# Bias loads placed behind weight loads, and a scan buffer returned later, in a two-layer hybrid backbone

## The chip, the cores and the metric

The kernel runs on one core of one Trainium2 chip. The metric is the device time of one execution in microseconds. Each of the runs shown is one execution; their median counts.

## The reference

Two layers work on 256 latent tokens and 256 context tokens of width 1024, all in float32. In each layer one projection of the modulated RMS norm feeds three mixers side by side: a bidirectional diagonal state-space scan (S5), a bidirectional chunked retention with four heads, and a neighbourhood attention with eight heads of 64. Each mixer has a projection of its own and a gate; the gated sum goes through an output projection and a residual, then a SwiGLU FFN follows. Of this the change touches two places. The attention adds a bias per head to the scores inside the window, before one softmax over window and context:

```python
s_win = jnp.einsum('bqhd,brqchd->bhqrc', q_r, k_win).astype(f32) + jnp.transpose(bias, (0, 2, 1, 3))[None]
s_ctx = jnp.einsum('bqhd,bkhd->bhqk', q_r, k_c).astype(f32)
s = jnp.concatenate([s_win.reshape(bsz, H, GRID_W, n_win), s_ctx], axis=-1)
p = jax.nn.softmax(s, axis=-1).astype(v.dtype)
```

The scan of S5 runs over the tokens in both directions and leaves complex states, real and imaginary part, which the readout multiplies.

## The kernel before

Weights come from DRAM as chunks of 128 x 1024 floats, in the order in which the program asks for them. `wraw` loads a chunk into one of four raw buffers in turn, from SyncE's (SP's) queue. `w` then splits it into two fp32r halves, `hi` by a cast on ScalarE (L387) and `lo` by a subtraction on VectorE (L388), in three buffers each. Every product of a projection is three matmuls (`mm3`, L393 to L395). The chunks of the adaLN weights (`ada`) are used as they are, by L526.

A layer is written as generators that `weave` mixes by counts: after each step of a main sequence it takes a set number of steps of side sequences. That fixes the order of the program. The order on each engine and in each queue is then laid out by a planner, which plays the program through with estimated times; `tc.issue_after(ins)` makes it put the instructions of a block behind `ins` on the engine of `ins`. All waits follow from the addresses that are written and read.

Addresses come from `Arena`, which is worked in the order of the program. A normal request takes the first free block behind a cursor that goes round; a request with `top=True` takes the highest block that fits. A buffer that is freed can be given out at once, and its new owner then waits for the old one's readers and writers.

In layer 0 the order is this. Projections of the attention for heads 0 to 3 run with the input of S5 beside them; those for heads 4 to 7 with the scan (`s5_scan`, GpSimd) and `attn(l, 0)`, the attention of heads 0 to 3. Then come the gates of branch 0 with `attn(l, 1)`, heads 4 to 7, and the gates of branch 2 with `s5_out`, the readout. Then `branch_mm(l, 2)` loads the stored gates into `tgm` buffers (L1692); `m_ret` makes the projections of the retention, with the rotary table `rope` (L1456), `s5_glu` and `ret_decay` beside it; and `branch_mm(l, 0)`, `gates(l, 1)` and `retention` follow. Layer 1 has another order of the same parts.

`attn` handles two pairs of heads, m = 0 and 1. For each head it loads the bias (L1397, 128 x 384 floats) into one of the four buffers made in `m_na`, which both halves of the heads share, and turns its sign on ScalarE (L1398). `softmax2` adds it on VectorE (L1334, L1335), takes exponentials on ScalarE (L1340, L1341) and scales (L1346). The result is transposed on PE (L1387), copied (L1411) and multiplied with the values (L1415).

`s5_scan` ends by exchanging halves of the states `X` through the buffer `swap`: two DMAs into it and two copies out of it on GpSimd (L1121, L1122). Layer 0 frees `swap`, `ug` and `X` together in `layer`, ahead of `branch_mm(l, 2)`. `s5_tables(1)` builds layer 1's S5 tables beside layer 0's `m_out`; `b2` is one of them.

Of the kernel before, what the change touches and what calls it, by code (L numbers as in the profile page):

```python
# [199 lines left out]
def mk(ap, off, dims):  # L200
    return bass.AP(ap.tensor, ap.offset + off, [list(ap.ap[0])] + [list(d) for d in dims])
# [29 lines left out]
def chain(*gens):  # L231
    for g in gens:
        yield from g


class Net:
# [451 lines left out]
    def s5_tables(self, l):  # L688

        nc, F = self.nc, self.F  # L690
        if l not in self.tabs:
            self.tabs[l] = F.alloc(1280, "p2", top=True), F.alloc(1040, "BB", top=True)
        P2, bb = (b.ap for b in self.tabs[l])
        for r in range(2):
            for ri in range(2):
                src = mk(self.PW[r * 64:r * 64 + 64], l * 32, [[64, 20], [2, 16], [1, 2]])
                dst = mk(P2[ri * 64:ri * 64 + 64], r * 2, [[64, 20], [4, 16], [1, 2]])
                nc.scalar.copy(dst, src)
        w1, w2 = self.swapped("s5b", l * 1024, 1024, F)
        b2, tm = F.alloc(1024, "b2"), F.alloc(1024, "bbt")  # L700
        f = [P2[:, (ri * 10 + 9) * 64:(ri * 10 + 10) * 64].unsqueeze(2).to_broadcast([P, 64, 16])
             for ri in range(2)]

        def v3(ap):
            return ap.rearrange("p (g h) -> p g h", h=16)

        nc.vector.memset(bb[:, 1024:1040], 0.0)
        for dst, a, b, op in ((bb[:, 0:1024], w1, w2, ALU.add), (b2.ap, w2, w1, ALU.subtract)):
            nc.vector.tensor_tensor(out=v3(dst), in0=v3(a.ap), in1=f[0], op=ALU.mult)
            nc.vector.tensor_tensor(out=v3(tm.ap), in0=v3(b.ap), in1=f[1], op=ALU.mult)  # L710

            x, y = (tm.ap, dst) if b is w2 else (dst, tm.ap)
            nc.vector.scalar_tensor_tensor(out=dst, in0=x, scalar=self.sgn[:, 0:1], in1=y, op0=ALU.mult, op1=op)
        for b in (w1, w2, tm):
            b.free()
        return b2
# [196 lines left out]
    def layer(self, l):  # L913
        nc, F = self.nc, self.F
        last = l == NL - 1
        n = self.nt = 256 if last else 512
        self.n0 = 512 - n
        na = [None, None]
        self.yna = self.yslot[0]
        if l == 0:  # L920
            self.ug = F.alloc(2048, "ug", top=True)
            mu = self.m_u(l)
            for qt in range(1, 4):
                next(mu)
                self.ada2(0, qt)
                next(mu)
                self.modulate(0, 0, [0, 1], self.rb0, 0, range(qt * 2, qt * 2 + 2))
            self.pfree(self.rb0)
            wdma = self.wdma
            for _ in mu:  # L930
                pass
            with self.tc.issue_after(wdma.ins), self.tc.issue_after(self.wdma.ins):
                nc.sync.dma_start(self.xsp, self.xb.ap)
            self.xb.free()
            b2 = self.s5_tables(0)
            ada = self.ada(0, (2, 3, 4, 5))
            self.adas = ada
            self.X = F.alloc(4 * 66 * 16, "X", top=True)
            kw = self.s5_kwins(0, True)
            e_in = chain(*(g for blk in range(4) for g in (self.s5_e(0, b2, blk), self.s5_in(0, blk))))  # L940
            weave(self.m_na(l, 0, na), (e_in, 3))
            self.log_gamma(self.s5in[:, 192:208])
            weave(self.m_na(l, 1, na), (self.s5_scan(l), 18), (self.attn(l, 0, na), 4), (self.take(ada, 5), 1),
                  (self.take(kw, 4), 1))
            weave(self.gates(l, 0, None), (self.attn(l, 1, na), 1.6), (self.take(ada, 5), 0.5), (kw, 0.5))
            weave(self.gates(l, 2, None), (self.s5_out(l, self.yslot[1]), 2), (self.take(ada, 5), 0.5))
            self.swap.free()
            self.ug.free()
            self.X.free()
            self.m = F.alloc(8 * n, "m", top=True)  # L950
            for _ in self.branch_mm(l, 2, None, self.yna, first=True):
                pass
            weave(self.m_ret(l), (self.s5_glu(l, self.yslot[1], self.yslot[0]), 0.8), (self.ret_decay(l), 0.75))
            self.yret = self.yslot[1]
            tg = F.alloc(8 * n, "tg", top=True)
            weave(chain(self.branch_mm(l, 0, None, self.yslot[0]), self.gates(l, 1, tg)), (self.retention(l), 2))
            self.x_alloc()
            nc.sync.dma_start(self.xb.ap, self.xsp)
            for _ in self.branch_mm(l, 1, tg, self.yret, final=True):
                pass  # L960
        else:
            self.norm(l, 0, [2, 3])
            nc.sync.dma_start(self.xsp, self.xb.ap)
            self.xb.free()
            for _ in self.e_left:
                pass
            for b in self.tabs[l]:
                b.free()
            self.ug = F.alloc(2048, "ug", top=True)
            self.X = F.alloc(4 * 66 * 16, "X", top=True)  # L970
            kpre = self.pair([("ws", l, O_NK + m * 128) for m in range(2)])
            for _ in self.m_u(l):
                pass
            weave(self.m_na(l, 0, na, kpre), (chain(*(self.s5_in(l, blk) for blk in range(4)), self.s5_scan(l)), 20))
            ada = self.adas
            weave(self.m_na(l, 1, na), (self.attn(l, 0, na), 2.5))
            self.yret = self.yslot[1]
            weave(self.m_ret(l), (self.attn(l, 1, na), 1.2), (self.ret_decay(l), 0.75))
            self.m = F.alloc(8 * n, "m", top=True)
            weave(self.branch(l, 2, self.yna, 0), (self.retention(l), 2.5))  # L980
            self.swap.free()
            tg = F.alloc(8 * n, "tg", top=True)
            ys5 = self.yslot[0][:, 1024:]
            weave(chain(self.branch(l, 1, self.yret, 1), self.gates(l, 0, tg)),
                  (chain(self.s5_out(l, self.yslot[0]), self.s5_glu(l, self.yslot[0], ys5)), 1))
            self.ug.free()
            self.X.free()
            self.x_alloc()
            nc.sync.dma_start(self.xb.ap, self.xsp)
            for _ in self.branch_mm(l, 0, tg, ys5, final=True):  # L990
                pass
        tg.free()
        self.m.free()
        ada = self.adas
        if last:
            ada = self.ada(1, (5,))
            for _ in self.m_out(l):
                pass
            F.cursor = 8192
            self.norm(l, 1, [2, 3])  # L1000
            self.fill(ada, 2, 1)
            weave(self.ffn(l), (ada, 0.5))
        else:
            e = []

            def ahead():
                self.tabs[1] = F.alloc(1280, "p2", top=True), F.alloc(1040, "BB", top=True)
                for blk in range(4):
                    self.et[blk] = F.alloc(2048, "et", top=True)
                b2 = self.s5_tables(1)  # L1010
                yield
                e.extend(self.s5_e(1, b2, blk) for blk in range(4))
                next(e[0])
                yield

            weave(self.m_out(l, lambda: self.norm(l, 1, [0, 1])), (ahead(), 0.5))
            self.norm(l, 1, [2, 3])

            def rest():
                yield from chain(e[0], e[1], e[2], self.s5_kwins(1))  # L1020
                next(e[3])

            self.adas = self.ada_sum(1, range(5))
            weave(self.ffn(l, lambda: self.norm(l + 1, 0, [0, 1])), (rest(), 0.5), (chain(ada, self.adas), 0.9))
            self.e_left = e[3]
        self.dump(f"xffn{l}", self.xT)
# [338 lines left out]
    def attn(self, l, half, na):  # L1365


        nc, F = self.nc, self.F
# [22 lines left out]
        for m in range(2):  # L1391
            out = self.misc()
            kh, kl, qh, ql = qk[m]
            bias = []
            for h in range(2):
                bias.append(self.biases[m * 2 + h])
                nc.sync.dma_start(bias[h].ap, self.I["nabias"][l, half * 4 + m * 2 + h])  # L1397
                nc.scalar.mul(bias[h].ap, bias[h].ap, -1.0)  # L1398
            val = lambda h, k: nv[:, k, (m * 2 + h) * 64:(m * 2 + h + 1) * 64]
            for qt in range(2):  # L1400
# [443 lines left out]
```

## Time and profile before

| | us |
|---|---|
| median of three runs | 1546.05 |
| fastest and slowest of them | 1538.01 and 1549.89 |
| the profiled execution | 1546.39 |
| its span, first to last instruction | 1544.6 |
| busy in the span: PE, VectorE, ScalarE, GpSimd | 1492.7, 984.1, 626.9, 259.5 |

The mean granted clock of PE over the span is 0.986 of full speed. DMA queues moved 255.35 MB, on average 165 GB/s. The profile names a line of the kernel (L387) for each group of instructions; PE is the matmul side of TensorE, PEld its loading of weights, DVE is VectorE, ACT ScalarE, POOL GpSimd. `fa` is the arena in which all float32 buffers lie, `ra` that of the split halves, `psall` PSUM. Times in rows are microseconds from the start of the span unless they are marked as ns.

### The profile page before, as it was taken

To read this page: it belongs to the slowest core of one execution; us is meant where nothing else is said; L and a number is where in the kernel's file an instruction comes from. 1 tells how busy PE (TensorE), PEld (TensorE's weight loads), DVE (VectorE), ACT (ScalarE), POOL (GpSimd) and SP (SyncE) were. 2 spreads that over 40 slices of the span, in tenths; PEclk is the share of its full clock that TensorE was granted. 3 is DMA by queue.
4 is the path that set the end of the run, shared out by engine and by line. 5 is a ranking of instruction groups with operands and counts; after the bars stand their busy time and mean duration, and the time that the engine had idled before them with its cause. 6 is when DMAs were issued, how large, how long until landed. Compare 5 with 4: busy or idle time off the path is not lost. (4 is left out here: it accounts for less than half of the span.)

```text
span 1544.6 us, 25494 instructions
## 1 busy us (share of the span) xinstructions
PE 1492.7 (97%) x10066; PEld 1269.3 (82%) x10066; DVE 984.1 (64%) x1729; ACT 626.9 (41%) x1121; POOL 259.5 (17%) x612
## 2 busy tenths in 40 slices
PE   7998898999999999999999999999999999999997
PEld 5886676788888888787887788898689899899997
DVE  6884754445356686598599974732565676665666
ACT  4554443334312334332322322454654355444443
POOL 6206996000000000000000000007991000000000
PEclk9999899999999999999999999999999999999999
DMA  9514456873332533455466642432325667555552
GB/s 369 190 55 141 159 208 176 278 258 113 123 102 69 164 96 111 167 186 178 153 205 214 230 160 65 157 123 75 101 83 161 230 225 271 179 192 184 171 190 98
DMA packets 80760, 255.35 MB, mean 165 GB/s; under 512 B 9216, under 2 KB 23040, under 8 KB 77824
## 3 DMA queue, kind: packets, MB, share of 16 engines
q1 hardware_dynamic: 78016, 247.36, 48.4%
q10 hardware_dynamic: 2304, 4.20, 0.8%
q0 software_dynamic: 320, 2.16, 0.6%
q8 instruction: 79, 1.29, 0.3%
q14 instruction: 41, 0.34, 0.1%
HBM read 230.68 MB, written 20.84 MB: 163 GB/s over the span
## 5 line engine op out<-in xcount | busy, mean ns | idle before, releaser
L393 PE MATMUL psall<-ra 128*128 128x256 f32 (+1 forms) x2122 | 711.3, 340 | 6.1 <-ACT ra L387 2.4
L394 PE MATMUL psall<-ra 128*128 128x256 f32 (+1 forms) x2122 | 709.0, 336 | 0.0
L395 PE MATMUL psall<-ra 128*128 128x256 f32 (+1 forms) x2122 | 707.4, 336 | 1.0 <-DVE ra L388 1.0
L388 DVE TENSOR_TENSOR ra<-fa,ra 128x1024 fp32r<-128x1024 f32 (+1 forms) x284 | 344.8, 1216 | 293.1 <-ACT ra L387 285.9
L387 ACT CAST ra<-fa 128x1024 fp32r<-128x1024 f32 (+1 forms) x284 | 293.7, 1038 | 557.9 <-PE psall L394 336.0
L393 PEld LDWEIGHTS psall<-ra 128*128 128x128 f32 x2122 | 401.7, 191 | 63.2 <-issue 10.7
L395 PEld LDWEIGHTS psall<-ra 128*128 128x128 f32 x2122 | 404.0, 191 | 44.9 <-issue 2.7
L394 PEld LDWEIGHTS psall<-ra 128*128 128x128 f32 x2122 | 405.2, 191 | 39.0 <-issue 1.3
L1109 POOL TENSOR_TENSOR fa<-fa 128x64 f32<-128x64 f32 x252 | 106.1, 442 | 137.4 <-ACT fa L1083 127.7
L1064 POOL MEMSET fa<- 128x32 f32 x2 | 0.2, 123 | 730.2 <-DVE ra L846 730.2
L570 DVE SCALAR_TENSOR_TENSOR fa<-fa 128x1024 f32<-128x1024 f32 x70 | 87.6, 1281 | 9.3 <-DMA fa<-in_wst_dram 7.6
L887 PE MATMUL psall<-ra 128*128 128x512 f32 x192 | 77.8, 414 | 0.2 <-ACT fa L1051 0.2
L888 PE MATMUL psall<-ra 128*128 128x512 f32 x192 | 76.2, 397 | 0.0
L1711 DVE SCALAR_TENSOR_TENSOR fa<-psall,fa 128x256 f32<-128x256 f32 x96 | 43.2, 480 | 51.3 <-PE psall L395 51.1
L889 PE MATMUL psall<-ra 128*128 128x512 f32 x192 | 75.3, 399 | 0.3 <-DVE ra L846 0.3
L1112 POOL TENSOR_TENSOR fa<-fa 128x64 f32<-128x64 f32 x126 | 58.2, 462 | 0.0
L1113 POOL TENSOR_TENSOR fa<-fa 128x64 f32<-128x64 f32 x126 | 53.8, 427 | 9.9
L887 PEld LDWEIGHTS psall<-ra 128*128 128x128 f32 x192 | 43.7, 229 | 8.0 <-issue 2.0
L889 PEld LDWEIGHTS psall<-ra 128*128 128x128 f32 x192 | 43.4, 229 | 6.5 <-DVE ra L846 0.8
L756 DVE TENSOR_TENSOR fa<-fa 128x1024 f32<-128x1024 f32 (+1 forms) x32 | 41.1, 1316 | 11.2 <-PE psall L1165 8.8
L888 PEld LDWEIGHTS psall<-ra 128*128 128x128 f32 x192 | 44.2, 230 | 4.9
L757 DVE TENSOR_TENSOR fa<-fa 128x1024 f32<-128x1024 f32 (+1 forms) x32 | 41.0, 1292 | 2.7 <-DMA fa<-in_s5c_dram 2.7
(242 smaller groups left out, 1380.5 us busy)
## 6 DMA issues: line engine op xcount, KB each, us to landing
fa<-in_wst_dram SPq DMA_DIRECT2D x364, 512.0 KB
gsp<-fa SPq DMA_DIRECT2D x8, 1152.0 KB
fa<-gsp SPq DMA_DIRECT2D x8, 1152.0 KB
fa<-in_wst_dram SPq DMA_DIRECT2D x16, 384.0 KB
xsp<-fa SPq DMA_DIRECT2D x2, 2048.0 KB
tgs<-fa ACTq DMA_DIRECT2D x16, 256.0 KB
fa<-kws SPq DMA_DIRECT2D x32, 128.0 KB
fa<-tgs SPq DMA_DIRECT2D x16, 256.0 KB
```

What stands on the lines that cost most here:

```text
L387: nc.scalar.copy(hi[:, :n], t[:, :n])
L388: nc.vector.tensor_tensor(out=lo[:, :n], in0=t[:, :n], in1=hi[:, :n].bitcast(F32), op=ALU.subtract)
L393: mm(out, wh, xh, start=start, stop=False)
L394: mm(out, wh, xl, start=False, stop=False)
L395: mm(out, wl, xh, start=False, stop=stop)
L570: nc.vector.scalar_tensor_tensor(out=acc[s].ap, in0=t, scalar=c, in1=acc[s].ap, op0=ALU.mult, op1=ALU.add)
L887: mm(o, xh, hi[:, ws], start=(kk == 0), stop=False)
L888: mm(o, xh, lo[:, ws], start=False, stop=False)
L889: mm(o, xl, hi[:, ws], start=False, stop=(kk == 7))
L1109: e.tensor_tensor(out=t[:, i], in0=at(pf, pr), in1=tab[:, i * 64:(i + 1) * 64].rearrange("p (r d g) -> p r d g", r=2, d=2), op=ALU.mult)
L1112: e.tensor_tensor(out=at(cf, cr), in0=at(cf, cr), in1=t[:, 0], op=ALU.add)
L1113: e.tensor_tensor(out=at(cf, cr), in0=at(cf, cr), in1=mk(T[s % 2], 96, [[-32, 2], [16, 2], [1, 16]]), op=ALU.add)
```

## The change

In `attn` the bias loads of the second half of the heads (`half` is 1) are put behind the weight load that the program issued last before them, `self.wdma`. In layer 0 the free of `swap` moves from ahead of `branch_mm(l, 2)` to behind the weave of `m_ret`, `s5_glu` and `ret_decay`. In `s5_tables` the buffer `b2` is taken from the top of the arena in layer 1.

```diff
-        b2, tm = F.alloc(1024, "b2"), F.alloc(1024, "bbt")
+        b2, tm = F.alloc(1024, "b2", top=l == 1), F.alloc(1024, "bbt")
...
             weave(self.gates(l, 2, None), (self.s5_out(l, self.yslot[1]), 2), (self.take(ada, 5), 0.5))
-            self.swap.free()
             self.ug.free()
             self.X.free()
...
             weave(self.m_ret(l), (self.s5_glu(l, self.yslot[1], self.yslot[0]), 0.8), (self.ret_decay(l), 0.75))
             self.yret = self.yslot[1]
+            self.swap.free()
             tg = F.alloc(8 * n, "tg", top=True)
...
                 bias.append(self.biases[m * 2 + h])
-                nc.sync.dma_start(bias[h].ap, self.I["nabias"][l, half * 4 + m * 2 + h])
+
+                with self.tc.issue_after(self.wdma.ins) if half else nullcontext():
+                    nc.sync.dma_start(bias[h].ap, self.I["nabias"][l, half * 4 + m * 2 + h])
                 nc.scalar.mul(bias[h].ap, bias[h].ap, -1.0)
```

## Rows read from the trace of the kernel before

**Rows 1.** The page: busy us (share of the span) xinstructions; DMA issues, KB each.

```profile
PE 1492.7 (97%) x10066; PEld 1269.3 (82%) x10066; DVE 984.1 (64%) x1729; ACT 626.9 (41%) x1121; POOL 259.5 (17%) x612
...
fa<-in_nabias_dram SPq DMA_DIRECT2D x16, 192.0 KB
```

**Rows 2.** Windows of layer 0: us, engines' busy us (xinstructions), granted PE clock, DMA share, GB/s.

```profile
120.00:280.00 160.00, 146.46 (x982) 104.41 (x980) 89.96 (x168) 67.41 (x174) 119.51 (x257) 0.95 0.56 179
200.00:260.00 60.00, 60.00 (x380) 43.51 (x379) 37.55 (x72) 25.34 (x67) 49.09 (x106) 1.00 0.61 203
280.00:580.00 300.00, 300.00 (x1775) 245.28 (x1774) 172.49 (x309) 101.79 (x152) 0.00 (x0) 1.00 0.45 147
580.00:600.00 20.00, 17.73 (x141) 14.89 (x139) 15.03 (x48) 9.93 (x19) 0.00 (x0) 0.87 0.43 136
```

**Rows 3.** PE's waits, 118 to 280: line <- releaser: us, times, longest.

```profile
PE psall L1415 <- ACT fa L1411: 4.4, 1, 4.4
PE psall L1387 <- DVE fa L1346: 3.5, 1, 3.5
PE psall L526 <- DMA fa<-in_wst_dram: 1.6, 1, 1.6
```

**Rows 4.** Windows over two stretches of half clock.

```profile
137.34:140.75 3.41, 3.41 (x20) 1.70 (x21) 0.00 (x0) 1.54 (x2) 3.02 (x11) 0.50 0.91 309
157.82:164.65 6.83, 6.83 (x18) 4.39 (x18) 6.76 (x13) 2.44 (x8) 6.36 (x11) 0.50 0.60 222
```

**Rows 5.** Waits of SP's queue, 118 to 180, and of its part to 134.

```profile
SPq L1397 <- DVE fa L1335: 19.8, 2, 12.8
...
SPq L683 <- DVE fa L1171: 3.8, 1, 3.8
...
SPq L377 <- PE psall L526: 0.2, 1, 0.2
```

**Rows 6.** Timeline of SP's queue, layer 0's attention: start, us, engine, line, issue.

```profile
132.34 0.33 SPq L1397 DMA_DIRECT2D fa<-in_nabias_dram  x1
132.98 0.33 SPq L377 DMA_DIRECT2D fa<-in_wst_dram  x1
133.75 0.33 SPq L1397 DMA_DIRECT2D fa<-in_nabias_dram  x1
...
151.68 1.28 SPq L377 DMA_DIRECT2D fa<-in_wst_dram  x3
...
168.50 0.33 SPq L1397 DMA_DIRECT2D fa<-in_nabias_dram  x1
...
185.07 12.40 SPq L377 DMA_DIRECT2D fa<-in_wst_dram  x2
```

**Rows 7.** Timeline of PE and ScalarE; in brackets the idle time before and its releaser.

```profile
137.34 1.08 PE L526 MATMUL psall<-fa 128*32 128x256 f32 x8 [1.62 <-DMA fa<-in_wst_dram]
...
138.49 0.52 ACT L1398 ACTIVATE fa<-fa 128x384 f32<-128x384 f32 x1 [1.18 <-DMA fa<-in_nabias_dram]
...
170.91 0.53 ACT L1398 ACTIVATE fa<-fa 128x384 f32<-128x384 f32 x1 [0.44 <-DMA fa<-in_nabias_dram]
```

**Rows 8.** Timeline of SP's queue and VectorE around heads 6 and 7.

```profile
225.78 14.08 SPq L377 DMA_DIRECT2D fa<-in_wst_dram  x4
...
243.75 0.47 DVE L1335 CUSTOM_DVE_ANT_0 fa<-psall,fa 128x256 f32<-128x256 f32 x1
...
246.84 6.51 SPq L1152 DMA_DIRECT2D fa<-kws  x3
```

**Rows 9.** Timeline: last copy out of `swap`, the rope load, the last readout matmuls.

```profile
267.91 1.94 POOL L1122 COPY fa<-fa 64x2112 f32<-64x2112 f32 x1
...
313.35 0.38 SPq L1456 DMA_DIRECT2D fa<-in_rope_dram  x1
...
319.68 2.83 PE L1227 MATMUL psall<-fa 128*32 128x128 f32 x96
```

**Rows 10.** Timeline of SP's queue in layer 1.

```profile
1065.59 18.20 SPq L377 DMA_DIRECT2D fa<-in_wst_dram  x5
1083.88 1.38 SPq L1397 DMA_DIRECT2D fa<-in_nabias_dram  x2
```

## Prediction

> **What bounds the kernel now.** I read the page first: TensorE (PE) is busy for 97% of the span, VectorE for 64%, ScalarE for 41% [rows 1]. So an edit can pay in two ways only: it shortens a stretch in which PE stands still, or one in which its clock is granted at half. The page's slices are too coarse to show where that is, so next I cut layer 0 into windows [rows 2]. From 280 to 580 us PE is busy for 300.00 of 300 us, at a granted clock of 1.00: nothing can be won there, only lost. From 200 to 260 us it is the same, 60.00 of 60. Over 120 to 280 us PE is busy for 146.46 of 160, so it stands for 13.5 us, all of them outside 200 to 260; from 580 to 600 us it stands for 2.3 us.
>
> Third come PE's waits in that part [rows 3]: the two longest, 4.4 and 3.5 us, are for ScalarE's L1411 and VectorE's L1346, not for a load. Of the other five one, 1.6 us, ends with a weight's landing. Fourth, the granted clock: behind these waits lie four stretches at 0.50, that is at 1.2 instead of 2.4 GHz. Three last 3.41 us and one 6.83 us [rows 4]; one of each is shown, and the one at 137.34 begins as PE resumes [rows 4, 7]. Half of 17.06 us is lost, 8.5 us. In all 13.5 + 8.5 = 22.0 us, 1.4% of the run: the most that a better order in this part of layer 0 could return.
>
> **The first edit: bias loads of heads 4 to 7 get a place in SP's queue behind a weight load.** There are eight, four in each layer. SP's queue is worked off in order, and in layer 0 it stood 19.8 us in two waits for such loads, 12.8 us before 132.34 and 7.0 us before 168.50 [rows 5, 6]. Each fills a buffer that VectorE's L1335 of the first four heads still reads. What matters is who stood behind it.
>
> Behind the load at 132.34 is a weight load at 132.98. It had to wait 0.2 us more for a release of its own, by PE's L526 [rows 5]: PE was still reading the old content of its buffer. So of the 12.8 us nothing was the bias load's doing. But its 192 KB [rows 1] go to the DMA engines ahead of that weight. They run at 0.91 of their time and 309 GB/s [rows 4], so these bytes take 197 KB / 309 GB/s = 0.64 us, and PE waits 1.62 us, until 137.34, for a weight [rows 7]. I take 0.64 us as won. Bounds: nothing, if another landing decides; or the whole 1.62 us and with it half of the 3.41 us at half clock that follow, 3.3 us together. I choose the row of bytes over the row of the wait since the weight itself has to land in the same stretch. The other load of this pair (133.75) stands behind that weight; ScalarE waits 1.18 us for it at L1398 [rows 7], while PE works for 3.41 of 3.41 us [rows 4]: 0.
>
> Behind the load at 168.50 comes a load of S5 tables that waited 3.8 us for VectorE's L1171 by itself [rows 5]: 0. The fourth load of layer 0 waits for nothing.
>
> The Trainium skill (DMA: Bandwidth & Descriptors, section "Anatomy of one DMA — SWDGE (gpsimd) path") says that the issuing sequencer takes a DMA's semaphore wait before dispatch. The trace agrees, with 12.8 us of standing queue. If all 19.8 us were worth their length, the time would be 1546.4 - 19.8 = 1526.6; the releases of the entries behind say otherwise.
>
> Where do the loads go? The anchor is the weight load issued last in the order of the program. For the first pair of layer 0 that is the first gate weight (gates, column 3584). Its raw buffer comes free when PE's L526 has read the ada chunk in it, so it is one of the three loads from 151.68. For the second pair it is the fifth gate weight, in the run of two loads that begins at 185.07 and ends at 197.5 [rows 6]. The second pair is the tighter: it is first read by L1335 at 243.75 [rows 8]. Landing took 170.91 - 168.50 = 2.4 us in one case and 138.49 - 133.75 = 4.7 in another [rows 6, 7]. So an issue at 197.5 leaves some 40 us. A pair in its new place costs, if cover is gone, its bytes ahead of weights, 2 x 0.64 = 1.3 us, and two issues of 0.33 us [rows 6], 2.0 us; for both pairs 4.0. PE's 60.00 of 60 us of work hide the second; before the first PE's next waits are for VectorE and ScalarE, not for weights. I take 0. Four sign changes on ScalarE (L1398, 0.52 us each [rows 7]) move along and are as many as before.
>
> In layer 1 the edge changes nothing. The first pair left at 1083.88, behind a run of weights from 1065.59 that holds its anchor [rows 10]; the other two loads stand likewise behind theirs. 0.
>
> **The second edit: the scan's exchange buffer (2112 columns) is held through m_ret.** By the arena's rules and the kernel's order of requests it lies at columns 8888 to 11000. In the kernel before, tgm buffers of branch_mm(l, 2) and then rg take that place. GpSimd leaves it at 267.91 + 1.94 = 269.9 [rows 9], and what takes it comes after s5_out: it held nobody up, so nothing is won. In the new layout six tgm buffers move up by 2296 columns, onto the attention's values and the low end of X, the scan's states. The rope table moves from 11776 to 14072, onto X. s5_out's last matmuls read X until 319.68 + 2.83 = 322.5; the rope load stood at 313.35 [rows 9]. It must leave 9.2 us later, or hold the queue for so long, with three weights behind it. At worst PE runs dry for all of it and a half-clock stretch of 6.83 us follows: 9.2 + 3.4 = 12.6 us. What hides it: three cast weights and four raw buffers ahead of a PE that has no gap here [rows 2], and rope is wanted only after the first projection of m_ret. I take 0, between bounds 0 and +12.6.
>
> **The third: b2 of layer 1's tables at the top.** It makes the room: with the second edit alone, a later request for 1152 columns finds no block. It also gives the scratch of the norm after layer 0's m_out other addresses. There, from 580 to 600 us, PE stands 2.3 us and the clock is 0.87 [rows 2], 2.6 us: 4.9 us is the bound either way. I take 0, since the norm is a chain of small steps in itself.
>
> **Sum.** 1546.39 (the profiled execution; its span is 1544.6, 1.8 lie around it; the median of three runs is 1546.05) - 0.64 + 0 + 0 = 1545.8.
>
> **Rivals.** *Nothing happens*: the landing that ends PE's wait at 137.34 is set elsewhere and the rest is covered, 1546.4. For it: seven of the eight loads hold up nobody.
>
> *Faster*: the order on every engine is laid out by planned times. With SP's queue no longer planned around two waits, 120 to 280 us gets another order, and the stalls go. All 22.0 us gives 1524.4; without the 6.83 us stretch, 1527.8. For it: these waits come from how attention and projections are interleaved, not from data that must be late. Against: the two long ones name engines and lines that no edit touches. The rule quoted above would end here too.
>
> *Slower*: the second pair of layer 0 comes too late. To land before L1398 (0.52 us) and L1335 at 243.75 it must be issued by 238.5 (landing 4.7) to 240.8 (landing 2.4). The weights from 225.78 to 239.86 hold the last slot. Behind them come the S5 windows, which hold the queue until 246.84 + 6.51 = 253.35 [rows 8]. Placed behind those, L1335 is 12.6 to 14.8 us late; ScalarE stands at L1398 with the casts of weights behind it, PE runs dry and then has 3.41 to 6.83 us at half clock: 14.3 to 18.2 us, some 1562. It decides if the issue slips past 240.8. Against: the two loads that waited left as soon as L1335 was done, so the plan puts such loads early.
>
> The Trainium skill (the same page, section "Rules for kernel authors") advises to issue a DMA early, compute, and wait for it late. This change does the reverse. The rows agree that cover shrinks, and leave some 40 us of it.
>
> **How the numbers follow.** Forecast 0.57, nothing 0.25, faster 0.10, slower 0.08. Around the first two an order that comes out otherwise may give or take half of the 22.0 us, 11 us, and a little for the rope: 1533 to 1558. One per cent, 15.5 us, is about what a measurement of this kernel can tell from no change. So faster 0.10, same 0.82, slower 0.08.
>
> **What would show it.** Right: no bias load on SP between 119 and 151 us; no wait of 12.8 us for L1335 there; PE's wait for a weight near 137 shorter by some 0.6 us; 280 to 580 still full; layer 1's bias loads where they were. Wrong: PE idle in 280 to 580; a PE wait of over 1 us for rope, tgm or a bias load; the two long waits gone, or new ones of their size, in 120 to 280; a bias load of layer 0 issued after 240.

## The result, and the profile after

The changed kernel takes 1553.72 us in the median of ten runs (1552.38 to 1562.61), the kernel before 1540.57 in ten runs beside it (1533.94 to 1549.89). The ratio, from all runs of the two, is 1.0077, with a 95% interval of 1.0058 to 1.0096: slower by 0.8%, or 11.9 us (the medians by themselves lie 13.2 us apart). The profiled execution takes 1552.5 us with a span of 1550.7. That of before took 1546.39, which is 5.8 above the median of its ten runs, so the two traces side by side show only 6.1 us; the rest has to come from more executions, and the experiments bring them.

First the windows of the changed kernel, those of [rows 2] and two more, which the next lines need (columns as in [rows 2]):

```profile
120.00:280.00 160.00, 144.23 (x958) 103.93 (x958) 91.72 (x166) 65.83 (x171) 119.44 (x257) 0.94 0.54 180
200.00:260.00 60.00, 58.63 (x360) 43.07 (x361) 35.05 (x66) 24.80 (x63) 49.35 (x109) 0.97 0.59 193
280.00:580.00 300.00, 300.00 (x1772) 245.38 (x1772) 172.38 (x308) 102.30 (x153) 0.00 (x0) 1.00 0.46 147
580.00:600.00 20.00, 17.71 (x155) 15.39 (x154) 15.39 (x49) 10.05 (x19) 0.00 (x0) 1.00 0.42 134
...
240.00:290.00 50.00, 46.95 (x360) 35.45 (x362) 20.92 (x39) 18.82 (x44) 15.00 (x26) 0.97 0.73 228
...
830.00:880.00 50.00, 42.81 (x231) 32.60 (x230) 40.76 (x46) 10.43 (x14) 0.00 (x0) 0.90 0.59 196
```

and the last two of them in the kernel before:

```profile
240.00:290.00 50.00, 45.58 (x348) 33.40 (x350) 20.92 (x44) 18.13 (x45) 16.11 (x26) 0.97 0.77 224
...
830.00:880.00 50.00, 47.39 (x265) 36.32 (x264) 45.98 (x52) 11.81 (x16) 0.00 (x0) 1.00 0.65 219
```

From 280 to 580 us PE is full in both. The place that stands out lies where the prediction never looked: from 830 to 880 us, in layer 0's FFN, PE works 42.81 us instead of 47.39 and the clock is 0.90 instead of 1.00. If the PE instructions of the two traces are set beside each other in order, the distance between them grows by some 8 us from 835 to 871 us and then stays within some 2 us to the end, where it is 6.1.

What happens there is seen in VectorE's timeline, here of the changed kernel (start, us, engine, line; in brackets the idle time before and its releaser; code lines behind L1397 are two higher than before, so L1713 is the residual L1711):

```profile
852.26 0.69 DVE L410 TENSOR_TENSOR ra<-fa,ra 128x512 fp32r<-128x512 f32 x1
857.30 2.63 DVE L756 TENSOR_TENSOR fa<-fa 128x1152 f32<-128x1152 f32 x2 [4.35 <-DMA fa<-in_s5c_dram]
859.85 0.87 DVE L1713 SCALAR_TENSOR_TENSOR fa<-psall,fa 128x256 f32<-128x256 f32 x2
860.64 1.35 DVE L757 TENSOR_TENSOR fa<-fa 128x1152 f32<-128x1152 f32 x1
861.90 1.22 DVE L388 TENSOR_TENSOR ra<-fa,ra 128x1024 fp32r<-128x1024 f32 x1
```

and of the kernel before:

```profile
852.21 0.69 DVE L410 TENSOR_TENSOR ra<-fa,ra 128x512 fp32r<-128x512 f32 x1
854.39 2.44 DVE L1711 SCALAR_TENSOR_TENSOR fa<-psall,fa 128x256 f32<-128x256 f32 x6 [1.50 <-PE psall L395]
856.75 1.22 DVE L388 TENSOR_TENSOR ra<-fa,ra 128x1024 fp32r<-128x1024 f32 x1
857.88 2.62 DVE L756 TENSOR_TENSOR fa<-fa 128x1152 f32<-128x1152 f32 x2
```

L756 is the first product of layer 1's last S5 window (`s5_g`), which the program builds beside layer 0's FFN. It waits for a load of `s5c` that leaves at nearly the same time in both kernels (854.8 and 855.0). Before, VectorE does the residuals and the subtraction L388 for the next weight first and meets a load that has landed. Now L756 stands ahead of them: VectorE is idle for 4.35 us, and L388, whose cast on ScalarE is done some 4 us before, waits for nothing but its turn and comes 5 us later than in the kernel before. PE waits for it:

```profile
849.53 1.49 PE L1165 MATMUL psall<-fa 128*32 128x128 f32 x30 [1.83 <-DVE fa L761]
851.98 1.94 PE L576 MATMUL psall<-fa 128*32 128x256 f32 x16 [0.96 <-DVE fa L1171]
863.17 0.50 PE L395 MATMUL psall<-ra 128*128 128x512 f32 x1 [4.39 <-DVE ra L388]
```

A second stall comes ahead of it: PE waits 1.83 us for L761, where in the kernel before a run of projection matmuls stood between. After each of the two the granted clock is at half, at 1.2 GHz:

```profile
850.13:856.96 6.83, 5.87 (x41) 3.51 (x32) 1.84 (x5) 2.10 (x5) 0.00 (x0) 0.50 0.74 294
863.78:867.19 3.41, 3.41 (x10) 2.64 (x9) 3.37 (x5) 0.49 (x1) 0.00 (x0) 0.50 0.72 198
```

PE stands 7.19 us in this window and loses half of 5.87 + 3.41 = 9.28 us, 4.64, to the clock: 11.8 us in all. In the kernel before it stands 2.61 there and loses nothing to the clock.

The second place is small in this pair of traces, and was found only through the first experiment. It is SP's queue at 246 us, in the changed kernel:

```profile
245.01 1.01 SPq L377 DMA_DIRECT2D fa<-in_wst_dram  x1
246.07 0.58 SPq L1152 DMA_DIRECT2D fa<-kws  x1
262.44 0.33 SPq L1694 DMA_DIRECT2D fa<-tgs  x1
262.87 7.08 SPq L377 DMA_DIRECT2D fa<-in_wst_dram  x5
```

Nothing leaves between 246.65 and 262.44. The waits of the queue from 240 to 275 us say why (us, times, longest):

```profile
SPq L1694 <- DMA fa<-fa: 11.7, 1, 11.7
SPq L1694 <- POOL fa L1122: 4.0, 1, 4.0
```

L1694 is a load of stored gates into a tgm buffer. It stands at the head of the queue while the scan's exchange (`fa<-fa`) runs, and until GpSimd has copied `swap` out at L1122; five weights stand behind it.

### The profile page after: what moved, and what is told of

It is laid out like the page before. It is cut to its first block, busy times and chain, and to the rows that moved or that the text cites. A ratio compares the mean times of both kernels' runs of the same rounds, so it can differ in the third digit from the quotient of the medians.

```text
span 1550.7 us, 25506 instructions
## 1 busy us (share of the span) xinstructions
PE 1492.9 (96%) x10066; PEld 1270.9 (82%) x10066; DVE 986.2 (64%) x1729; ACT 625.8 (40%) x1121; POOL 257.5 (17%) x612
## 4 chain that ended last, share of the span: by engine, by line
PE 88%; DVE 4%; DMA 2%; ACT 2%; POOL 2%; issue 1%; SPq 0%; DVEq 0%; ACTq 0%; POOLq 0%
PE psall L393 23%; PE psall L394 23%; PE psall L395 23%; PE psall L887 3%; PE psall L889 2%; PE psall L888 2%; PE psall L1075 1%; PE psall L1227 1%; PE psall L1380 1%; PE psall L1417 1%; PE psall L1387 1%; PE psall L526 1%; DMA fa<-in_wst_dram 1%; PE psall L1589 1%; DMA fa<-in_nabias_dram 1%
## 5 line engine op out<-in xcount | busy, mean ns | idle before, releaser
L388 DVE TENSOR_TENSOR ra<-fa,ra 128x1024 fp32r<-128x1024 f32 (+1 forms) x284 | 344.0, 1213 | 297.9 <-ACT ra L387 284.6
L387 ACT CAST ra<-fa 128x1024 fp32r<-128x1024 f32 (+1 forms) x284 | 293.5, 1038 | 543.7 <-PE psall L394 318.1
L1713 DVE SCALAR_TENSOR_TENSOR fa<-psall,fa 128x256 f32<-128x256 f32 x96 | 43.4, 479 | 48.2 <-PE psall L395 47.9
L756 DVE TENSOR_TENSOR fa<-fa 128x1024 f32<-128x1024 f32 (+1 forms) x32 | 40.8, 1311 | 16.0 <-PE psall L1165 8.8
L409 ACT CAST ra<-fa 128x512 fp32r<-128x512 f32 (+1 forms) x52 | 26.5, 510 | 38.9 <-DVE fa L1779 26.4
```

The lines of the kernel that those rows point to most:

```text
L387: nc.scalar.copy(hi[:, :n], t[:, :n])
L388: nc.vector.tensor_tensor(out=lo[:, :n], in0=t[:, :n], in1=hi[:, :n].bitcast(F32), op=ALU.subtract)
```

## The experiments

Two stages tell the kernels apart. For each the table gives what PE loses in it, in the one profiled execution of that kernel: the time it stands, and half of its busy time at half clock. The third column is the stage ahead of them.

| kernel | ratio, 95% interval | 120–240 us | 240–290 us | 830–880 us |
|---|---|---|---|---|
| before | 1 | 15.7 | 6.1 | 2.6 |
| changed | 1.0077 (1.0058–1.0096) | 19.8 | 4.8 | 11.8 |
| e1_bias | 0.9969 (0.9948–0.9990) | 14.9 | 0.0 | 2.3 |
| e2_arena | 1.0077 (1.0054–1.0101) | 14.3 | 7.6 | 12.3 |
| e3_b2 | 1.0000 (0.9978–1.0023) | 16.9 | 6.8 | 2.6 |
| e4_fix | 1.0059 (1.0037–1.0082) | 19.4 | 8.0 | 5.8 |
| e5_tgs | 1.0022 (1.0001–1.0044) | 15.6 | 0.0 | 12.3 |
| e6_cur | 1.0022 (1.0002–1.0042) | 18.9 | 7.5 | 2.3 |
| e7_tgscur | 0.9976 (0.9954–0.9998) | 17.0 | 0.0 | 2.3 |
| e8_bias_again | 0.9965 (0.9946–0.9983) | 19.4 | 0.1 | 2.4 |
| e9_m0 | 0.9983 (0.9962–1.0004) | 18.1 | 0.4 | 2.7 |
| e10_m1 | 0.9993 (0.9971–1.0015) | 14.4 | 5.3 | 2.3 |

### The edits one by one

**e1_bias**, the first edit alone:

```diff
+                with self.tc.issue_after(self.wdma.ins) if half else nullcontext():
+                    nc.sync.dma_start(bias[h].ap, self.I["nabias"][l, half * 4 + m * 2 + h])
```

> The first edit alone (second-half bias loads behind weights), swap and b2 as before. Theory A, the loss comes from the order in layer 0's FFN, which follows from the returned swap buffer: no loss here, ratio to before 0.998 to 1.002; VectorE makes the residuals L1711 and the subtraction L388 ahead of the products L756 near 855 us, PE's wait there stays about 1 us and the granted clock of 840 to 880 us stays 1.00. Theory B, the loss comes from the bias loads (stalls in 120 to 280 us): ratio 1.006 to 1.009, and PE's waits and half clock in 120 to 280 us are over 22 us by 8 or more.

Measured: 0.9969 (0.9948 to 0.9990), faster by 0.31%, 4.8 us. Theory B is out. Theory A said too little: I had expected no difference, and the edit gains. The gain lies from 240 to 290 us, where PE now doesn't stand at all and the clock is 1.00:

```profile
240.00:290.00 50.00, 50.00 (x431) 38.05 (x434) 20.02 (x39) 20.36 (x45) 17.58 (x36) 1.00 0.84 257
```

**e2_arena**, the second and third edit:

```diff
-        b2, tm = F.alloc(1024, "b2"), F.alloc(1024, "bbt")
+        b2, tm = F.alloc(1024, "b2", top=l == 1), F.alloc(1024, "bbt")
...
-            self.swap.free()
             self.ug.free()
...
             self.yret = self.yslot[1]
+            self.swap.free()
```

> Second and third edit (swap freed later, b2 from the top), bias loads as before. Theory A: the whole loss, ratio 1.005 to 1.010; near 857 us L756 stands ahead of the residual on VectorE and waits over 3 us for the s5c load, PE waits over 3 us for L388, and the clock drops to half in 845 to 870 us for 6 us or more in all. Theory B: ratio 0.998 to 1.002.

Measured: 1.0077 (1.0054 to 1.0101), the ratio of the whole change. L756 waits 4.66 us for the load and PE 4.99 us for L388. So the loss is in these two edits, and what the first edit gains is missing in the whole change.

**e3_b2**, the third edit alone:

```diff
-        b2, tm = F.alloc(1024, "b2"), F.alloc(1024, "bbt")
+        b2, tm = F.alloc(1024, "b2", top=l == 1), F.alloc(1024, "bbt")
```

> Third edit alone (b2 of layer 1 from the top). The order of every engine and queue is that of the kernel before; only addresses differ. Theory A (order decides, an address by itself costs nothing): ratio 0.999 to 1.001, and the trace differs from that of before only by chance, so it also shows how far two executions of one order differ. Theory C (the addresses themselves cost, through waits on the buffers underneath): ratio 1.005 or more, with waits of VectorE or SP in 590 to 870 us that the kernel before doesn't have.

Measured: 1.0000 (0.9978 to 1.0023). By the arena's rules seventeen buffers lie elsewhere, and nothing comes of it. By subtraction the loss belongs to the late `swap`, which has no room without this edit, or to the two together.

**e4_fix**, the changed kernel with the last block's products behind the residual:

```diff
+        with self.tc.issue_after(self.res.ins) if l and blk == 3 else nullcontext():
+            self._prods(gb.ap, c1.ap, c2.ap, 0, l, blk, 9, ALU.subtract, F, self.sgn[:, 1:2])
```

> The changed kernel with one wait more: the products of layer 1's last block in s5_g (L756, L757, L761) are put behind the residual that the program issued last before them on VectorE. Theory A: the wait of PE for L388 near 859 us falls from 4.4 us to about 1 us and its half clock of 3.4 us behind it goes; the stall of 1.8 us at 848 us and its half clock of 6.8 us stay, since nothing of them is touched. So 3.4 + 1.7 = 5.1 us come back of the loss of about 12: ratio to before about 1.004 (1.002 to 1.006). Theory B: nothing comes back, ratio 1.007 to 1.009.

At its place it does what was expected. VectorE has the residual and L388 first again (one more code line here: the residual is L1714):

```profile
861.87 0.88 DVE L1714 SCALAR_TENSOR_TENSOR fa<-psall,fa 128x256 f32<-128x256 f32 x2 [3.44 <-PE psall L395]
862.66 1.22 DVE L388 TENSOR_TENSOR ra<-fa,ra 128x1024 fp32r<-128x1024 f32 x1
```

The wait for L388 is gone, the 1.83 us for L761 with its half clock stay, and the stage loses 5.8 us instead of 11.8. The ratio, 1.0059 (1.0037 to 1.0082), is inside the expected range at its upper end, but its interval overlaps that of the changed kernel: the time alone decides nothing here. The profiled execution loses 8.0 us from 240 to 290, and this pointed to the second place.

### The two consequences of the late `swap`

Compared PE instruction by PE instruction, e1_bias and the changed kernel have the same order up to some 470 us; yet 4.7 us of the distance between them arise from 262 to 273 us. On ScalarE the cast L387 waits there for a weight in the changed kernel and for nothing of the sort in e1_bias (first the changed kernel, then e1_bias):

```profile
266.80 1.04 ACT L387 CAST ra<-fa 128x1024 fp32r<-128x1024 f32 x1 [7.60 <-DMA fa<-in_wst_dram]
...
268.24 0.58 ACT L1413 COPY fa<-psall 128x512 f32<-128x512 f32 x1
```

```profile
259.04 1.05 ACT L387 CAST ra<-fa 128x1024 fp32r<-128x1024 f32 x1 [3.00 <-PE psall L394]
...
260.52 0.59 ACT L1413 COPY fa<-psall 128x512 f32<-128x512 f32 x1
```

Behind the cast stands the copy L1413, and for that PE waits 3.1 us at L1417, with 3.41 us at half clock behind it. The weight is late because it stands behind the gate load, and the gate load stands there because of `swap`. By the arena's rules the columns 8888 to 11000 lie idle from the exchange until `swap` is returned ahead of `tg`; then the first to use a part of them for a load is a tgm buffer of branch 0 (columns 9400 to 9912). That load waits for the exchange and for nothing later, so the planner finds it ready at its planned end of the exchange, and puts it ahead of weights. In the kernel before, the same request gets columns 1536 to 2048, on buffers of the stage of `m_ret`, so its load has the last readers of those to wait for.

The next four kernels test this against the FFN's order, each alone and both together.

**e5_tgs**, the changed kernel with branch 0's gate loads behind a weight:

```diff
+                with self.tc.issue_after(self.wdma.ins) if l == 0 and gi == 0 else nullcontext():
+                    nc.sync.dma_start(tb.ap, self.tgs[gi * 8 + mt])
```

> The changed kernel with the gate loads of branch 0 (L1694, into tgm) put behind the weight load that the program issued last before them. The order of all engines stays that of the changed kernel; only SP's queue differs: the gate load that stood from 246 to 262 us behind the exchange's last copy (L1122) goes back behind the weights of branch 0. Theory A (two separate losses: this gate load at the head of SP's queue, and VectorE's order in layer 0's FFN): SP issues weights between 246 and 262 us, ScalarE's cast L387 no longer waits 7.6 us for a weight, PE's wait of 3 us for L1413 near 266 us and the half clock of 3.4 us behind it go, some 8 us less at 287 us than in the changed kernel; the 8 us of 848 to 870 us stay. Ratio to before 1.001 to 1.004. Rival (only the FFN costs, the early gate load is harmless): 1.006 to 1.009.

**e6_cur**, the changed kernel with the cursor put back ahead of layer 1's tables:

```diff
+                F.cursor = 4152
                 b2 = self.s5_tables(1)
```

> The changed kernel with the arena's cursor set, ahead of layer 1's S5 tables, to the place where it stood there in the kernel before. From there on every buffer has the address it has when the third edit is made alone, and VectorE, ScalarE, GpSimd and PE have the order of the first edit alone in layer 0's output projection and FFN; the early gate load on SP stays. Theory A: L756 stands behind the residuals again, the waits of 1.8 and 4.4 us on PE and both half clock stretches of 845 to 870 us go, about 8 us; the loss near 246 to 287 us stays. Ratio to before 1.001 to 1.004. Rival (the place of the buffers doesn't set the order's cost): 1.006 to 1.009.

**e7_tgscur**, both:

> Both of these together: swap is still freed late, but its two consequences are taken away. Theory A: the two add up, ratio to before 0.995 to 0.999, that of the first edit alone. Rival (something else in the second edit costs, rope's load or the rest of the order of 300 to 560 us): 1.002 or more.

**e8_bias_again**, the first edit alone once more:

> The first edit alone once more, on the same chip as the three kernels that take consequences of the second edit away. Theory A: ratio 0.995 to 0.999, not told apart from the kernel with both consequences taken away. Its gain, if it is one of order, shows at 246 to 287 us again: ScalarE's cast L387 doesn't wait 10 us for a weight there, and PE has no wait over 2 us between 255 and 275 us. Rival (the gain of the first run was chance): ratio 0.9995 to 1.002.

Measured: 1.0022 (1.0001 to 1.0044), 1.0022 (1.0002 to 1.0042), 0.9976 (0.9954 to 0.9998) and 0.9965 (0.9946 to 0.9983). By the ratios e7 is 0.46%, 7.1 us, below e5 and as much below e6 (by the medians 8.7 and 7.1 us). Both together on top of e7 make 1.0068, and the changed kernel has 1.0077 (1.0058 to 1.0096). So the two consequences add up, they are all that the late `swap` costs within the intervals, and without them the first edit's gain is there.

Against the kernel before, the early gate load is hardly a loss in itself. From 240 to 290 us that kernel loses 6.1 us, and the kernels with the late `swap` and this gate load lose 4.8 to 8.0. It takes back what the first edit gains; what is added to the kernel before is the loss in the FFN.

In e5 SP has its weights out in time:

```profile
245.72 16.62 SPq L377 DMA_DIRECT2D fa<-in_wst_dram  x5
262.45 1.84 SPq L1152 DMA_DIRECT2D fa<-kws  x3
```

and PE loses nothing from 240 to 290; L756 still stands ahead, and 12.3 us go from 830 to 880. In e6 it is the other way round. The gate load stands until 263.64, and VectorE has the order of the kernel before (the gate load is L1695 here, the residual L1714):

```profile
263.64 0.33 SPq L1695 DMA_DIRECT2D fa<-tgs  x1
264.07 7.00 SPq L377 DMA_DIRECT2D fa<-in_wst_dram  x5
```

```profile
856.55 2.44 DVE L1714 SCALAR_TENSOR_TENSOR fa<-psall,fa 128x256 f32<-128x256 f32 x6 [1.52 <-PE psall L395]
858.91 1.21 DVE L388 TENSOR_TENSOR ra<-fa,ra 128x1024 fp32r<-128x1024 f32 x1
860.04 2.62 DVE L756 TENSOR_TENSOR fa<-fa 128x1152 f32<-128x1152 f32 x2
```

One number in the arena's bookkeeping, set ahead of tables that VectorE begins at 546 us, some 300 us ahead of the stall, decides this order. It moves no work and no edge of the data; it decides which old buffer lies under which new one. That the order follows since the planner then believes steps of the S5 windows ready at other times is how the planner works, and wasn't followed step by step.

### What the first edit gains

In the kernel before, ScalarE's cast waits even longer than in the changed kernel:

```profile
267.87 1.04 ACT L387 CAST ra<-fa 128x1024 fp32r<-128x1024 f32 x1 [10.16 <-DMA fa<-in_wst_dram]
```

The last two weights that left SP ahead of that moment stood behind three loads L1152, which took 6.51 us to issue [rows 8], and left while the exchange was in flight:

```profile
253.45 5.94 SPq L377 DMA_DIRECT2D fa<-in_wst_dram  x2
```

In e1_bias the loads L1152 have gone by 243.3, and five weights follow. The edit's two halves were to put this to the test.

**e9_m0** and **e10_m1**, the first edit for one pair of heads each:

```diff
+                with self.tc.issue_after(self.wdma.ins) if half and m == 0 else nullcontext():
```

> The first edit for the pair m = 0 alone (the second half's other pair of bias loads as before). SP's order after the last pair of bias loads: near 245 to 262 us three weights and then five stand with three loads L1152 between them, where the kernel before has two weights, three loads L1152, two weights and three loads L1152 more. Theory D, the first edit gains because ScalarE's cast L387 near 258 us no longer waits 10 us for a weight behind loads L1152 and the exchange: this kernel shows the gain, PE has no wait over 2 us from 255 to 275 us, ratio to before 0.994 to 0.998. Rival E, the gain comes from the bias loads themselves (SP's 19.8 us of waits at L1397 taken away, mostly those of the pair m = 1): ratio 0.999 to 1.002 here.

> The first edit for the pair m = 1 alone. SP's order near 245 to 265 us is that of the kernel before (two weights, three loads L1152, two weights, three loads L1152). Theory D: the wait of ScalarE's cast L387 for a weight (about 10 us) and PE's wait of some 4 us for L1411 near 266 us with half clock behind it stay; ratio 0.999 to 1.003. Rival E: the gain is here, 0.994 to 0.998.

The waits of ScalarE from 240 to 275 us, first e9, then e10 (us, times, longest):

```profile
ACT ra L387 <- PE psall L394: 7.5, 3, 3.0
```

```profile
ACT ra L387 <- DMA fa<-in_wst_dram: 9.2, 1, 9.2
ACT ra L387 <- PE psall L394: 8.1, 2, 4.9
```

As theory D says, the wait for the weight is gone where the pair m = 0 is moved, and stays where m = 1 alone is; PE loses 0.4 us from 240 to 290 in the one and 5.3 in the other. The ratios, 0.9983 (0.9962 to 1.0004) and 0.9993 (0.9971 to 1.0015), don't tell the two apart, and e9 falls short of the 0.998 that was expected at the most: 120 to 240 us cost 18.1 us there and 14.4 in e10. So that this stall is the gain of the first edit is shown by the traces at its place; that the pair m = 0 alone keeps it is not shown by the times.

Nor could the two times have told D from rival E. E gave most of the 19.8 us of SP's waits to the pair m = 1, but 12.8 of them, those before 132.34, are of the pair m = 0 [rows 5, 6], so by E too the gain would belong into e9. What speaks against E is the queue itself. In the changed kernel SP stands as long in that stretch, now for a weight's own buffer (waits from 118 to 180 us; 2.2 us in the kernel before):

```profile
SPq L377 <- PE psall L526: 18.9, 4, 13.4
```

The weight that the cast waits for isn't held up in SP's queue. In e10, where the wait is 9.2 us, the last weights that leave ahead of the cast are out by 252.5, and the cast starts at 264.74:

```profile
250.90 1.56 SPq L377 DMA_DIRECT2D fa<-in_wst_dram  x2
```

So the weight was at least 12 us on its way, with the exchange in flight for most of it: GpSimd's copy L1121, which waits for that, starts at 264.03. Whether the bytes of the loads L1152 ahead of it or those of the exchange made it late wasn't separated and stays open. So does how the place of two bias loads near 130 us comes to change SP's order at 240.

## Why the prediction was right or wrong

The time was forecast at 1545.8 us, between 1533 and 1558, and within 1% of before. It came out at 1553.7, inside both. The direction was wrong: a hair faster was forecast, and the interval of the ratio lies above 1. That the time lies inside the range is luck: its 11 us up and down were meant for another order in 120 to 280 us, and what is added to the kernel before lies at 830 to 880. Nor is one per cent what a measurement here can tell; the interval of the ratio is 0.2% to either side. By the prediction's own steps:

**What bounds the kernel** held. 280 to 580 us is full, and the gains and losses that were found are stalls of PE and stretches at half clock. But the windows that were cut in layer 0 ended at 600 us, since no line of the edits seemed to touch anything later there.

**The first edit** was sized by a wait that differs by as much between executions. PE's wait for the weight near 137 us fell from 1.62 us [rows 3] to 1.03:

```profile
PE psall L526 <- DMA fa<-in_wst_dram: 1.0, 1, 1.0
```

0.59 us, for which 0.64 was taken; but the match is luck. Without the edit the wait is 0.7 us in e2_arena, and e3_b2, with the order of the kernel before on every engine, has none; with the edit it lies between none (e7_tgscur) and 1.05 us (e5_tgs). The anchors were named rightly. The first pair leaves at 148.85, behind its weight, which itself leaves 3.7 us earlier than the 151.68 of before, so that the sign "no bias load on SP between 119 and 151 us" was missed by 2 us. The second pair leaves at 184.33, near the 185.07 that was named, and layer 1's leave behind the same run of weights (1090.02 for 1083.88 [rows 10], late by the 6.1 us of the rest):

```profile
148.85 0.90 SPq L1399 DMA_DIRECT2D fa<-in_nabias_dram  x2
...
184.33 1.71 SPq L1399 DMA_DIRECT2D fa<-in_nabias_dram  x2
...
1090.02 1.38 SPq L1399 DMA_DIRECT2D fa<-in_nabias_dram  x2
```

A step that failed is the price of nothing for the first pair's new place, with the reason that PE's next waits there "are for VectorE and ScalarE, not for weights". ScalarE is where the bias load is wanted. Its sign change (L1400 here) stands ahead of the exponential L1340 in ScalarE's order:

```profile
155.76 0.52 ACT L1400 ACTIVATE fa<-fa 128x384 f32<-128x384 f32 x1 [2.30 <-DMA fa<-in_nabias_dram]
...
156.79 1.64 PE L1380 MATMUL psall<-ra 64*128 64x512 f32 x3 [3.18 <-ACT fa L1340]
```

VectorE has what L1340 needs ready at 152.9, L1340 starts right behind the sign change at 156.19, and PE stands 3.18 us for it. The changed kernel and e1 and e4 to e8 all have this wait of PE, of 1.1 to 3.2 us; the four kernels in which the first pair stands as before (before, e2, e3, e10) have one of 1.4 us for VectorE there instead. In e9 the loads have landed when ScalarE comes to them. The second pair holds ScalarE too, for 5.61 us until 188.97, since the 40 us of cover were counted to VectorE's L1335; no wait of PE for it is to be seen.

As a whole the term was mis-sized: 4.8 and 5.4 us gained by the two ratios (0.31% and 0.35%) instead of 0.6, in spite of that wait. The step that failed for the gain is the sentence that the two long waits "name engines and lines that no edit touches". The 4.4 us at L1415 named ScalarE's copy L1411 [rows 3]. That copy was late because the cast ahead of it on ScalarE waited 10.16 us for a weight, and the weight stood in the queue that the edit rearranges. A releaser is the last link; what the releaser's own engine waited for before it would have led to SP. So it was the mechanism of the rival "faster" (another order, the stalls go), for one of the two long stalls and with about a quarter of its 22.0 us; the rest of the change hid it.

**The second edit** was right about what moves off: the rope load leaves at 322.45, as it had to, and costs nothing, since the stretch is full:

```profile
322.45 0.42 SPq L1458 DMA_DIRECT2D fa<-in_rope_dram  x1
```

It failed in the sentence "it held nobody up, so nothing is won". I had asked who is displaced, and not who comes next into the place that is held longer. That was a gate load with one early condition, and the planner pulled it forward to stand 15.7 us at the head of SP's queue. Measured: 7.1 us between e6 and e7, with a bound of 12.6 but from another cause. And it failed in its list of what moves. It named six tgm buffers and the rope table; by the arena's rules 158 of 669 buffers get other addresses, among them those of layer 1's S5 tables and what follows. That gave VectorE the order that costs 7.1 us by the ratios, 8.7 by the medians, between e5 and e7, in the FFN. The prediction had nothing for it.

The Trainium skill (DMA: Bandwidth & Descriptors, section "Rules for kernel authors") advises to issue a DMA early and wait late. This load is the case in which early costs, as it had its own wait to stand out at issue: e5 issues it later and is faster than the changed kernel. For the first pair of bias loads the trace agrees with the advice: issued later, they make PE wait up to 3.18 us.

**The third edit** was right alone, 1.0000. The prediction did see that other addresses may cost, but bounded it by the norm at 580 to 600 us, where it changes little: 17.71 us busy for 17.73, with no half clock this time. The failed step of both is to take the reach of moved addresses to end with the first buffers that move: the cost came in the FFN, 250 us behind the norm.

**The rivals.** "Slower" had the right sign with the wrong mechanism: the second bias pair did not slip. Its price, some 16 us for a weight and a cast held up, is the kind of price that was paid, twice and at half the size.

**What would show it** served well in two lines. "New ones of their size, in 120 to 280": there are three waits of 3.1 to 3.2 us there in the changed kernel for the 4.4 and 3.5 of before. "A PE wait of over 1 us for rope, tgm or a bias load": two of these three are such waits, by way of ScalarE, the one at 156.79 for a bias load and the one at L1417 for a weight behind a tgm load.

The first edit alone beats both kernels, 0.9969 and 0.9965; keeping `swap` longer brought nothing that the runs show.

## What to carry to other kernels

Where a planner lays out the order from addresses, an edit of a buffer's life reaches as far as the arena's cursor does: list which new buffers lie on which old ones in every later stage with small margins, and look first for loads that lose their late condition and can be pulled ahead in an in-order queue. Undo such side effects one by one, with an anchor for the load or a fixed cursor, before judging the edit. And when a wait names an engine, read what that engine itself waited for just before. In the same way count the cover of a load that is moved to the first engine that has to stand for it, not to the engine that reads it for the work.

## What the runs showed of the hardware

The same order can cost several microseconds more or less from one execution to the next. The changed kernel and the kernels e1 and e4 to e8 have one order on every engine and in SP's queue from 120 to 240 us, and lose from 14.9 to 19.8 us there; e1_bias and e8_bias_again, which are the same kernel, lose 14.9 and 19.4. A part of this can be followed to a DMA. The wait of PE for L1340 that was shown above for the changed kernel, 3.18 us, is 1.11 us long in e1_bias:

```profile
155.20 0.52 ACT L1400 ACTIVATE fa<-fa 128x384 f32<-128x384 f32 x1 [0.49 <-DMA fa<-in_nabias_dram]
...
156.23 1.65 PE L1380 MATMUL psall<-ra 64*128 64x512 f32 x3 [1.11 <-ACT fa L1340]
```

The load that ScalarE waits for left SP at 150.54 in e1_bias and at 149.33 in the changed kernel: the same 192 KB are there after 4.7 us in the one and after 6.4 in the other. PE's clock is at 0.50 for 6.83 us from 154.31 on in e1_bias, and for 10.24 us in the changed kernel:

```profile
153.81:164.05 10.24, 7.26 (x19) 4.75 (x20) 8.00 (x14) 3.59 (x11) 9.61 (x19) 0.50 0.64 239
```

So two single traces differ by as much as many an edit is worth; that the profile of before lay 5.8 us above its median hid half of this change's loss.
